# Input projections of ten column chunks as block products: seven products for eight

## The chip, the cores and the metric

The kernel runs on one core of one Trainium2 chip. A core has a tensor engine for matmuls (PE; its weight loads are listed as PEld), a vector engine (VectorE, DVE), a scalar engine (ScalarE, ACT), GpSimd (POOL) and SyncE (SP), which here issues nearly all transfers. Each engine runs its own instructions in a fixed order. Matmuls add up in eight banks of PSUM, of 512 fp32 numbers in each of 128 partitions; everything else lies in SBUF. The metric is the device time of one execution in microseconds.

## The reference

One layer of an encoder runs over two independent inputs with shared weights: a prompt of 512 tokens and a sample of 1024 tokens, 1024 features each, all in fp32. Cut to what matters here:

```
h = rmsnorm(x) ; z = h @ w_in                    # 1024 -> 512 q, 128 k, 128 v, 512 ca, 512 cb
a = window_attention(q, k, v, bias, sink)        # |q - k| <= 128
c = silu(layernorm(dwconv31(ca * sigmoid(cb))))  # over tokens, per channel
x = x + concat(a, c) @ w_out
u = dwconv3(rmsnorm(x) @ w_up)                   # 1024 -> 2 * 2816
x = x + (silu(u[:, :2816]) * u[:, 2816:]) @ w_down
y = rmsnorm(x)
```

The change concerns `z = h @ w_in` alone.

## The kernel before

**Numbers and tiles.** Every fp32 operand of a matmul is split in two: a leading part that ScalarE rounds to the format the tensor engine reads, and the remainder. A product is then three matmuls (leading by leading, leading by remainder, remainder by leading), each of 128 x 128 weights against 512 tokens. `split` makes the two parts of a weight chunk: ScalarE casts, GpSimd subtracts.

**The input projection.** The 1792 columns of `w_in` are 14 chunks of 128 columns. The tokens are three groups of 512: group 0 is the prompt, groups 1 and 2 are the halves of the sample. The activations come in transposed, x times the norm's gain is split by `raw_h1` (a cast on ScalarE, the remainder on VectorE) into `h1[group]`, and the norm's scale of each token is applied later, when a result leaves PSUM (`row_scale` makes it, `rbs` holds it). A step, one chunk for one group, is 8 blocks of 128 features by 3 matmuls, 24 in all (`proj`), after which `landed` and `evac` take the result out of its bank: VectorE scales it, and by its kind (q, k, v, ca, cb) it goes to the attention's buffers or to the input of the depthwise convolution.

**Order of the work.** `order` lists the chunks in two passes. In the first, the first two chunks (cb and ca of channel chunk 0) are done for all three groups as the data arrive (`beside`, line 526). Chunks 2 and 3 (channel chunk 1) follow for all three groups, and the ten others (k, v, four of q, and cb and ca of channel chunks 2 and 3) for group 0 alone. In the second pass these ten chunks are loaded and split again, for groups 1 and 2, while the prompt's attention runs beside them. Then come the prompt's output projection, its feed-forward part with the sample's attention beside it, the sample's output projection, its up-projection and the down-projection.

The prompt's convolutions run beside the first pass, mainly as a chain of 26 VectorE instructions for each channel chunk that multiply and add into one PSUM bank (`taps`, line 352), with four taps given to ScalarE and GpSimd. They are emitted by `tick`, which is called four times in a step: each call gives a credit (`CA`, 0.9 us in the first pass, `CB`, 0.4 us in the second), and a tap costs 0.663 us of credit. The side work of the second pass, the prompt's attention, is paced in the same way by a rate per tick (`RB`).

**What sets the order.** The text of the kernel gives each instruction its place in the program. A planner simulates the engines and gives each engine, whenever it is free, the earliest instruction in the program whose inputs and buffer are ready; that fixes the order of each engine's instructions. Late parts of the kernel have the tensor engine's order written out by hand (`manual_schedule`); the parts touched here do not. Buffers are slots of fixed sizes (`Slots`: classes q of 4096 bytes, h of 2048 and others), given out in the order of the program, oldest released first. The PSUM banks go the same way.

**The scheme that is there already.** The sample's up-projection (`prod`, `sums_up`, `split_up`, from line 1156) computes a product of 2 x 2 blocks with seven block products in place of eight: sums and differences of blocks are made on VectorE, and results are combined in PSUM by copying a bank into another as its starting value and adding further products to it. [...]

The lines that the change touches: 40 (`RB`), 122 (slots), 170 to 173 (`order`), 478 (`raw_h1`), 508 (`step`), 537 (`load_xT(2)`), 583 to 616 (the first pass), 897 to 905 (the second pass) and 1810 (the program's set-up).

Of the kernel before, what the change touches and what calls it, by code (L numbers as in the profile page):

```python
# [15 lines left out]
P = 128  # L16
# [22 lines left out]

RA, RB, RBO, RD, RN, RE = 1.2, 0.8, 2.5, 0.55, 0.8, 0.9  # L40

# [67 lines left out]
def tile_hybrid_encoder(ctx: ExitStack, tc: tile.TileContext, xs, rel_bias, norm_attn_g, w_in,  # L109
# [19 lines left out]
    def bank(job):  # L129
        return banks.tile([NT], among=use[job])  # L130
# [40 lines left out]
    npr = len(order)  # L171
    order += kv_ + qs + cs[2] + cs[3]
    nch = len(order)
    raws, ws = {}, {}

# [73 lines left out]
    lng, lnb, fb = vecs[:, 20:24], vecs[:, 24:28], vecs[:, 28:72]  # L249

    def square_sum(x, ss, k):
        junk = sb.tile([D], BF16, 2)
        if k % 2 == 0:
            nc.scalar.activation(junk[:], x[:], AF.Square, accum_out=ss)
        else:
            nc.vector.tensor_tensor_reduce(out=junk[:], in0=x[:], in1=x[:], scale=1.0, scalar=0.0,
                                           op0=ALU.mult, op1=ALU.add, accum_out=ss)

    def spread(rs, job):
        wide_rs = sb.tile([4, P])  # L260
        for i in range(4):
            nc.scalar.activation(wide_rs[:, i, :], ident[:], AF.Identity, scale=0.0, bias=rs[:, i:i + 1])
        pt = bank(job)
        for i in range(4):
            nc.tensor.transpose(pt[:, i * P:(i + 1) * P], wide_rs[:, i, :], ident[:])
        return pt
# [128 lines left out]
    def evac(kind, c, nt, src):  # L395
# [55 lines left out]
        else:  # L451
            vs = sb.tile([NT])
            nc.vector.tensor_tensor(vs[:], src, rb[:], op=ALU.mult)
            pt = bank("step")
            for i in range(4):
                nc.tensor.transpose(pt[:, i * P:(i + 1) * P], vs[:, i * P:(i + 1) * P], ident[:])
# [20 lines left out]

    def raw_h1(nt, kc):
        t, m = xq.pop((nt, kc))
        x, hi, lo = t[:, m, :], sb.tile([NT], F32R), sb.tile([NT], F32R)  # L480
        nc.scalar.activation(hi[:], x, AF.Identity, scale=gA[:, kc:kc + 1])
        nc.vector.scalar_tensor_tensor(lo[:], x, gA[:, kc:kc + 1], hi[:].bitcast(F32), op0=ALU.mult, op1=ALU.subtract)
        h1.setdefault(nt, []).append((hi, lo))

    def first_pieces():
        ws[0], ws[1] = [(Halves([]), Halves([])) for _ in range(2)]
        for (k0, n), w in zip(PIECES, first_w):
            hi, lo = sb.tile([n, 2 * P], F32R), sb.tile([n, 2 * P], F32R)
            for kc in range(k0, k0 + n):
                raw_h1(0, kc)  # L490
# [17 lines left out]
    def step(i, nt):  # L508
        kind, c, col = order[i]
        pp = bank("step")  # L510
        proj(pp[:], ws[i], h1[nt])
        landed(i, nt, pp)
# [23 lines left out]
    nc.sync.dma_start(cvw[:, :CK * 4], laid["cvw"])  # L536
    drawn(load_xT(2))
    want_raw(2)
# [9 lines left out]
    for kc in range(KC):  # L548
        raw_h1(1, kc)

# [32 lines left out]
    pace.update(rate=RA, conv=CA, late=0)  # L583
    NALL = 4
    for nt in range(3):
        if nt:
            pps.update({(nt, c): bank("step") for c in range(2)})
            for kc in range(KC):
                beside(nt, kc)
        if nt == 1:  # L590
            for kc in range(KC):
                raw_h1(2, kc)
            want_w(2)
            row_scale(1)
            want_raw(3)
            drawn(load_rows(2))
            constants()
        if nt == 2:
            row_scale(2)
            want_w(3)  # L600
        for i in range(2):
            landed(i, nt, pps.pop((nt, i)))
    for i in range(2):
        ws.pop(i)
    for i in range(2, npr):
        want_raw(i + 2)
        want_w(i + 1)
        for nt in range(3 if i < NALL else 1):
            step(i, nt)
        ws.pop(i)  # L610
        if i == 2:
            bbd = bias_to_dram()
        if i == BL:
            load_bias(2)
    drain(side)
    h1.pop(0)
    rbs.pop(0)
    blocks = [(G, b) for G in GR for b in range(G["nb"])]
# [1211 lines left out]
```

## Time and profile before

| what | value |
|---|---|
| median of 3 runs | 1486.21 us (1485.44 to 1487.02) |
| the profiled execution | 1484.85 us, its span 1483.1 us |
| busy: PE, PEld | 1468.5, 1212.0 us |
| busy: VectorE, ScalarE, GpSimd | 1118.2, 805.5, 770.7 us |
| mean granted clock of the tensor engine | 0.998 |
| chunks 0 and 1 (L526) | 4.9 to 39.3 us |
| first and second pass, other chunks (L315 to L317) | 39.3 to about 264 us |

In the answers of the profile an instruction stands with its line, engine and operation, the tile it writes and those it reads (`h<-q` writes a tile of slot class h and reads one of class q; a, b, c and u are PSUM banks), and its shape. A group shows the count, the busy time and the mean duration in ns, then the idle time of the engine just before these instructions and what ended it. In an order of time the first two numbers are start and duration in us, and a count behind x joins neighbours of one kind. A wait shows who waited for whom, the total in us, how often, and the longest.

### The profile page before, as it was taken

Reading aid. Unit: us, or ns where it says so; the run is one execution under the profiler, and the core shown is the slowest. Engines: PE = TensorE matmul, PEld = TensorE weight load, DVE = VectorE, ACT = ScalarE, POOL = GpSimd, SP = SyncE. Lnnn points to the kernel's source line nnn. Section 1 sums busy time; section 2 is a strip of 40 time slices with the busy share of each in tenths; the row PEclk is TensorE's granted clock in tenths of the full one; section 3 lists DMA queues with packets and bytes.
Section 4 is the critical chain, followed back from the end, with each engine's and each line's share of the span. In section 5 each row is a group of like instructions: output and inputs, shape, how many; then the busy total and the mean of one; then the engine's idle time right before and its main releaser. Section 6 shows DMA issues by size and latency. Waiting matters only on the chain.

```text
span 1483.1 us, 19870 instructions
## 1 busy us (share of the span) xinstructions
PE 1468.5 (99%) x6736; PEld 1212.0 (82%) x6736; DVE 1118.2 (75%) x1510; ACT 805.5 (54%) x1424; POOL 770.7 (52%) x689
## 2 busy tenths in 40 slices
PE   9999999999999999999999999999999999999998
PEld 7788887878888888788888888888888888888886
DVE  6877945648988888676868888888886856578774
ACT  7524555567778776653465545445544553433355
POOL 3564453338779766322336666666654251135546
PEclk9999999999999999999999999999999999999999
DMA  9554331844444454663214443333332494356644
GB/s 367 200 151 146 102 107 29 263 142 142 127 137 136 134 178 142 201 225 108 71 58 142 135 135 128 127 130 128 123 126 87 152 326 167 124 188 220 224 163 163
DMA packets 124626, 228.19 MB, mean 154 GB/s; under 512 B 20420, under 2 KB 45764, under 8 KB 124397
## 3 DMA queue, kind: packets, MB, share of 16 engines
q1 hardware_dynamic: 124092, 226.37, 46.6%
q8 instruction: 53, 0.87, 0.2%
q10 hardware_dynamic: 432, 0.56, 0.1%
q14 instruction: 49, 0.39, 0.1%
HBM read 166.83 MB, written 61.10 MB: 154 GB/s over the span
## 4 chain that ended last, share of the span: by engine, by line
PE 89%; DVE 3%; DMA 3%; ACT 2%; POOL 2%; issue 1%; SPq 0%; POOLq 0%; DVEq 0%; ACTq 0%
PE w L1194 8%; PE w L1196 8%; PE w L1195 8%; PE w L1528 7%; PE w L1527 7%; PE w L1526 7%; PE b L315 4%; PE b L317 4%; PE b L316 4%; PE u L315 4%; PE u L317 4%; PE u L316 4%; PE a L692 1%; PE a L650 1%; PE u L796 1%; PE u L798 1%
## 5 line engine op out<-in xcount | busy, mean ns | idle before, releaser
L163 POOL TENSOR_TENSOR q<-q,q 128x1024 fp32r<-128x1024 f32 x66 | 159.2, 2412 | 66.9 <-ACT q L162 42.8
L1074 POOL TENSOR_TENSOR q<-q,q 128x512 fp32r<-128x512 f32 x81 | 116.5, 1445 | 119.4 <-ACT q L1180 117.1
L1074 DVE TENSOR_TENSOR h<-h,h 128x512 fp32r<-128x512 f32 (+1 forms) x152 | 131.9, 897 | 57.6 <-ACT h L1082 23.4
L1526 PE MATMUL w<-h,h 128*128 128x512 f32 x432 | 168.0, 389 | 0.0
L1528 PE MATMUL w<-h,h 128*128 128x512 f32 x432 | 168.0, 389 | 0.0
L1527 PE MATMUL w<-h,h 128*128 128x512 f32 x412 | 160.3, 389 | 0.0
L1194 PE MATMUL w<-h,q 128*128 128x512 f32 x368 | 144.3, 392 | 0.7 <-ACT w L1267 0.4
L1196 PE MATMUL w<-h,q 128*128 128x512 f32 x368 | 143.2, 389 | 0.0
L1195 PE MATMUL w<-h,q 128*128 128x512 f32 x347 | 135.0, 389 | 0.0
L1074 POOL TENSOR_TENSOR h<-h,h 128x512 fp32r<-128x512 f32 (+1 forms) x38 | 53.5, 1411 | 142.4 <-ACT h L1509 117.5
L1082 ACT CAST h<-h 128x512 fp32r<-128x512 f32 x116 | 69.3, 620 | 104.4 <-DVE h L1074 25.8
L315 PE MATMUL b<-h,q 128*128 128x512 f32 x312 | 123.0, 395 | 1.4 <-ACT h L461 0.8
L317 PE MATMUL b<-h,q 128*128 128x512 f32 x312 | 122.5, 393 | 0.0
L316 PE MATMUL b<-h,q 128*128 128x512 f32 x312 | 122.3, 392 | 0.0
L315 PE MATMUL u<-h,q 128*128 128x512 f32 x272 | 106.8, 393 | 0.0
L316 PE MATMUL u<-h,q 128*128 128x512 f32 x272 | 106.8, 393 | 0.0
L317 PE MATMUL u<-h,q 128*128 128x512 f32 x272 | 106.7, 392 | 0.0
L162 ACT CAST q<-q 128x1024 fp32r<-128x1024 f32 x66 | 69.1, 1048 | 52.1 <-PE u L316 16.8
L352 DVE SCALAR_TENSOR_TENSOR c<-d,cvw,c 128x512 f32<-128x512 f32 x128 | 96.0, 750 | 1.6
L344 POOL TENSOR_TENSOR h<-h,h 128x512 f32<-128x512 f32 x62 | 81.6, 1318 | 27.5 <-ACT h L343 23.0
L1526 PEld LDWEIGHTS w<-h,h 128*128 128x128 f32 x432 | 81.1, 188 | 16.8
L1528 PEld LDWEIGHTS w<-h,h 128*128 128x128 f32 x432 | 81.1, 188 | 16.7
(474 smaller groups left out, 3990.3 us busy)
## 6 DMA issues: line engine op xcount, KB each, us to landing
q<-in_laid_w_up SPq DMA_DIRECT2D x88, 512.0 KB, 3.7
ga<-q SPq DMA_DIRECT2D x65, 256.0 KB, 2.2
h<-gap SPq DMA_DIRECT2D x57, 256.0 KB, 3.5
h<-ga SPq DMA_DIRECT2D x57, 256.0 KB, 3.5
h<-in_w_down SPq DMA_DIRECT2D x52, 256.0 KB, 3.4
q<-in_laid_w_in SPq DMA_DIRECT2D x22, 512.0 KB, 3.9
gap<-h SPq DMA_DIRECT2D x44, 256.0 KB, 3.2
q<-in_x_sample SPq DMA_DIRECT2D x15, 512.0 KB, 7.5
```

Of the source, the lines that this page charges most:

```text
L163: (nc.vector if dve else nc.gpsimd).tensor_tensor(lo[:], raw[:], hi[:].bitcast(F32), op=ALU.subtract)
L315: nc.tensor.matmul(out, whi[:, kc, :], hi[:], start=(kc == 0), stop=False)
L316: nc.tensor.matmul(out, whi[:, kc, :], lo[:], start=False, stop=False)
L317: nc.tensor.matmul(out, wlo[:, kc, :], hi[:], start=False, stop=(kc == KC - 1))
L352: nc.vector.scalar_tensor_tensor(acc[:], src(t), w(t), acc[:], op0=ALU.mult, op1=ALU.add)
L1074: (eng or nc.vector).tensor_tensor(out, a, b, op=ALU.subtract)
L1194: nc.tensor.matmul(out, whi[:, s], hi[:], start=(start and c == 0), stop=False, **go)
L1195: nc.tensor.matmul(out, whi[:, s], lo[:], start=False, stop=False, **go)
L1196: nc.tensor.matmul(out, wlo[:, s], hi[:], start=False, stop=(stop and c == 3), **go)
L1526: nc.tensor.matmul(out, sh[:, c], th[:], start=(p == 0 and not seeded), stop=False, **go)
L1527: nc.tensor.matmul(out, sh[:, c], tl[:], start=False, stop=False, **go)
L1528: nc.tensor.matmul(out, sl[:, c], th[:], start=False, stop=(p == NPAIR - 1), **go)
```

## The change

The ten chunks 4 to 13 become five pairs (k and v; q 0 and 1; q 2 and 3; cb and ca of channel chunk 2; of 3). For each pair the 2 x 2 blocks are: the two halves of the 1024 features, the two chunks, and the two token groups 0 and 1. `block_pair` computes the four results of a pair (two chunks for two groups) with seven block products of 4 x 3 matmuls.

- `x_sums` and `x_split` make the sums of x once: per feature block a difference on GpSimd, a scaling on ScalarE and three instructions on VectorE, then casts on ScalarE and remainders on GpSimd (on VectorE for operand 7). Products 1, 2 and 4 take parts of `h1` as they are. This stands between the four plain steps of chunks 2 and 3 and in the first pair.
- `w_sums` and `w_split` make the sums of a pair's weights (four instructions on VectorE) and split the seven operands (seven casts on ScalarE, seven remainders on GpSimd, of 512 elements), one pair ahead.
- `seeded` copies a bank into another by ScalarE as its starting value, with an additional matmul if the bank is in `cut_banks`, that is, if it was last cleared by a transpose.
- Group 2 leaves the first pass. Its loads move: the rows for the norm to the third pair, the transposed activations to the last, where `raw_h1` splits them. The second pass does all 14 chunks for group 2 only, 14 steps; four more chunks of weights are loaded and split again.
- `load_bias` moves behind the pairs. `RB` goes from 0.8 to 1.15. Seven slots of class h are added, and the set-up reserves less memory for descriptors of transfers.

The core of the diff:

```diff
-RA, RB, RBO, RD, RN, RE = 1.2, 0.8, 2.5, 0.55, 0.8, 0.9
+RA, RB, RBO, RD, RN, RE = 1.2, 1.15, 2.5, 0.55, 0.8, 0.9
-               dict(q=(15, 4096), c=(4, 4352), h=(61, 2048), d=(2, 2304), s=(33, 64)))
+               dict(q=(15, 4096), c=(4, 4352), h=(68, 2048), d=(2, 2304), s=(33, 64)))
-    order += kv_ + qs + cs[2] + cs[3]
+    order += kv_ + qs + cs[0] + cs[1] + cs[2] + cs[3]
+    PLAIN = 4
+    pairs = [(i, i + 1) for i in range(PLAIN, npr, 2)]
...
+    def x_sums(c):
+        g1, g2 = gA[:, c:c + 1], gA[:, HK + c:HK + c + 1]
+        x11, x21, x12, x22 = x_of(0, c), x_of(0, HK + c), x_of(1, c), x_of(1, HK + c)
+        d = xsum[7, c] = sb.tile([NT])
+        nc.gpsimd.tensor_tensor(d[:], x11, x12, op=ALU.subtract)
+        nc.scalar.activation(x12, x12, AF.Identity, scale=g1)
+        nc.vector.scalar_tensor_tensor(x12, x22, g2, x12, op0=ALU.mult, op1=ALU.add)
+        nc.vector.scalar_tensor_tensor(x11, x11, g1, x12, op0=ALU.mult, op1=ALU.subtract)
+        nc.vector.scalar_tensor_tensor(x21, x21, g2, x11, op0=ALU.mult, op1=ALU.add)
...
+    def w_sums(p):
+        if p < len(pairs):
+            g0, g1, v0, v1 = (w_block(i, k) for i in pairs[p] for k in range(2))
+            t = wthird[p] = sb.tile([NT])
+            tt = nc.vector.tensor_tensor
+            tt(t[:], v1, v0, op=ALU.subtract)
+            tt(v0, v0, g0, op=ALU.subtract)
+            tt(g0, v0, v1, op=ALU.subtract)
+            tt(g1, g1, g0, op=ALU.add)
...
+    def block_prod(out, p, i, start):
+        whi, wlo = wops.pop((p, i))
+        for c in range(HK):
+            hi, lo = xop[i, c]
+            s = slice(c * P, (c + 1) * P)
+            nc.tensor.matmul(out, whi[:, s], hi[:], start=(start and c == 0), stop=False, **go)
+            nc.tensor.matmul(out, whi[:, s], lo[:], start=False, stop=False, **go)
+            nc.tensor.matmul(out, wlo[:, s], hi[:], start=False, stop=(c == HK - 1), **go)
+            if c == 1:
+                tick()
+        tick()
...
+    def seeded(src):
+        out = bank("step")
+        if out.slot[0] in cut_banks:
+            hi, lo = xop[5, HK - 1]
+            nc.tensor.matmul(out[:], hi[:, 0:P], hi[:], start=True, stop=True)
+            cut_banks.discard(out.slot[0])
+        nc.scalar.copy(out[:], src[:])
+        return out
...
+    def block_pair(p):
+        a, b = pairs[p]
+        last = p == len(pairs) - 1
+        w_load(p + 2)
+        X = started()
+        block_prod(X[:], p, 1, True)
+        Y = seeded(X)
+        if p == 0:
+            for c in range(HK):
+                x_split(7, c)
+            w_split(p, 7)
+        else:
+            w_split(p + 1, 1, 2)
+            w_sums(p + 1)
+        block_prod(X[:], p, 2, False)
+        if last:
+            drawn(load_xT(2))
+        landed(a, 0, X)
...
+        block_prod(Y[:], p, 6, False)
+        u = sb.tile([NT])
+        nc.scalar.copy(u[:], Y[:])
...
+        Z = started()
+        block_prod(Z[:], p, 5, True)
+        p5 = sb.tile([NT])
+        nc.scalar.copy(p5[:], Z[:])
+        w_split(p + 1, 7)
+        block_prod(Y[:], p, 7, False)
+        V = seeded(Y)
+        nc.vector.tensor_tensor(Y[:], Y[:], p5[:], op=ALU.add)
...
+        block_prod(Z[:], p, 3, False)
+        nc.vector.tensor_tensor(Z[:], Z[:], u[:], op=ALU.add)
...
+        block_prod(V[:], p, 4, False)
+        landed(a, 1, V)
+        landed(b, 0, Z)
+        landed(b, 1, Y)
...
-    for i in range(2, npr):
-        want_raw(i + 2)
-        want_w(i + 1)
-        for nt in range(3 if i < NALL else 1):
-            step(i, nt)
-        ws.pop(i)
+    w_load(0)
+    for n, (i, nt) in enumerate(((2, 0), (2, 1), (3, 0), (3, 1))):
+        if n == 2:
+            w_split(0, 1, 2)
+            w_sums(0)
+        x_sums(n)
+        for k in (6, 5):
+            x_split(k, n)
+        step(i, nt)
...
+    w_split(0, 6, 5)
+    for p in range(len(pairs)):
+        if p == len(pairs) - 3:
+            drawn(load_rows(2))
+            row_scale(2)
+        block_pair(p)
+    load_bias(2)
...
-        for nt in range(1, 3):
-            step(i, nt)
+        step(i, 2)
...
-    nc = _bacc.Bacc("TRN2", target_bir_lowering=False, num_devices=1)
+    nc = _bacc.Bacc("TRN2", target_bir_lowering=False, num_devices=1, dynamic_dma_scratch_size=1024)
```

More of the change, by code (lines that the diff above doesn't have):

```diff
@@ L249, in tile_hybrid_encoder @@
     lng, lnb, fb = vecs[:, 20:24], vecs[:, 24:28], vecs[:, 28:72]
+    cut_banks = {f[0] for f in banks.free}
     def square_sum(x, ss, k):
@@ L263, in spread @@
         pt = bank(job)
+        cut_banks.add(pt.slot[0])
         for i in range(4):
@@ L454, in evac @@
             pt = bank("step")
+            cut_banks.add(pt.slot[0])
             for i in range(4):
@@ L548, in tile_hybrid_encoder, with pair_tile, x_of @@
     for kc in range(KC):
-        raw_h1(1, kc)
+        raw_h1(1, kc, True)
+    HK = KC // 2
+    xop, wops, wdone, wthird = {}, {}, set(), {}
+    def pair_tile():
+        if sum(f[0][0] == "q" for f in sb.free) > 6:
+            both = sb.tile([2, NT], F32R, among="q")
+            return Part(both, 0), Part(both, 1)
+        return sb.tile([NT], F32R), sb.tile([NT], F32R)
+    xsum = {}
+    def x_of(nt, kc):
+        t, m = xq[nt, kc]
+        return t[:, m, :]
+    def x_sums(c):
[7 more added lines that the diff above has]
+        nc.vector.scalar_tensor_tensor(x21, x21, g2, x11, op0=ALU.mult, op1=ALU.add)
+        xq.pop((1, HK + c))
@@ new lines, in x_split @@
+    def x_split(i, c):
+        hi, lo = xop[i, c] = pair_tile()
+        if i == 7:
+            src, g = xsum.pop((7, c))[:], gA[:, c:c + 1]
+            nc.scalar.activation(hi[:], src, AF.Identity, scale=g)
+            nc.vector.scalar_tensor_tensor(lo[:], src, g, hi[:].bitcast(F32), op0=ALU.mult, op1=ALU.subtract)
+            return
+        key = {5: (1, c), 6: (0, c), 3: (0, HK + c)}[i]
+        src = x_of(*key)
+        nc.scalar.copy(hi[:], src)
+        nc.gpsimd.tensor_tensor(lo[:], src, hi[:].bitcast(F32), op=ALU.subtract)
+        xq.pop(key)
@@ new lines, in w_split @@
+    def w_split(p, *which):
+        if p >= len(pairs):
+            return
+        a, b = pairs[p]
+        for i in which:
+            if i == 7:
+                held = wthird.pop(p)
+                src = held[:]
+            else:
+                src = w_block(*{1: (a, 0), 2: (a, 1), 6: (a, 0), 4: (a, 1), 5: (b, 0), 3: (b, 1)}[i])
+            if any(f[0][0] == "q" for f in sb.free):
+                t = sb.tile([2, NT], F32R, among="q")
+                hi, lo = Part(t, 0), Part(t, 1)
+            else:
+                hi, lo = sb.tile([NT], F32R), sb.tile([NT], F32R)
+            wops[p, i] = hi, lo
+            nc.scalar.copy(hi[:], src)
+            nc.gpsimd.tensor_tensor(lo[:], src, hi[:].bitcast(F32), op=ALU.subtract)
+            held = None
+            wdone.add((p, i))
+        for chunk, two in ((a, (6, 4)), (b, (5, 3))):
+            if chunk in raws and all((p, i) in wdone for i in two):
+                raws.pop(chunk)
@@ new lines, in block_prod @@
+    def block_prod(out, p, i, start):
+        whi, wlo = wops.pop((p, i))
+        go = dict(skip_group_check=not start)
+        for c in range(HK):
[4 more added lines that the diff above has]
+            nc.tensor.matmul(out, wlo[:, s], hi[:], start=False, stop=(c == HK - 1), **go)
+            if p == len(pairs) - 1:
+                xop.pop((i, c))
+            if c == 1:
+                tick()
+        tick()
```

93 lines of the change are left out of this document (65 added, 28 removed).

## The prediction

> **What bounds the kernel now.** I read the page first, then the tensor engine in order of time, then busy time by stretch, then the groups of instructions in the stretch that the change rebuilds.
>
> ```profile
> PE 1468.5 (99%) x6736; PEld 1212.0 (82%) x6736; DVE 1118.2 (75%) x1510; ACT 805.5 (54%) x1424; POOL 770.7 (52%) x689
> PE 89%; DVE 3%; DMA 3%; ACT 2%; POOL 2%; issue 1%; SPq 0%; POOLq 0%; DVEq 0%; ACTq 0%
> L526 PE MATMUL a<-h,h 128*128 128x512 f32 x48 | 11.0, 389 | 0.0
> 17.04 11.04 PE L526 MATMUL a<-h,h 128*128 128x512 f32 x48
> ```
>
> The tensor engine is busy for 1468.5 of 1483.1 us and carries 89% of the chain, so a matmul fewer is time saved, if the others keep up. What one is worth is not its duration. The last line is 48 matmuls back to back in 11.04 us; one alone lasts 0.389 us, so the pitch is (11.04 - 0.389) / 47 = 0.2266 us. I count with the pitch.
>
> ```profile
> 0.00:17.00 17.00, 15.32 (x64) 11.88 (x65) 8.90 (x13) 12.08 (x19) 7.50 (x22) 1.00 0.89 315
> 25.60:69.00 43.40, 42.73 (x191) 34.13 (x191) 39.06 (x58) 26.01 (x46) 20.45 (x17) 1.00 0.66 247
> 128.00:264.00 136.00, 133.45 (x653) 110.40 (x652) 90.43 (x182) 73.34 (x163) 60.41 (x77) 1.00 0.30 87
> 830.00:1100.00 270.00, 270.00 (x1190) 222.53 (x1189) 228.35 (x199) 134.46 (x200) 168.97 (x127) 1.00 0.40 131
> 1470.00:1483.10 13.10, 7.25 (x32) 5.66 (x31) 2.79 (x3) 2.95 (x7) 3.50 (x4) 0.86 0.57 220
> ```
>
> Columns: the stretch, its length, busy time of PE, PEld, DVE, ACT and POOL with their instructions, granted clock, DMA share, GB/s. The clock is 1.00 in all that the change touches. The tensor engine loses 1.7 us at the start and 5.9 at the end; elsewhere it hardly waits. But from 25.6 to 69.0 us the vector engine is busy for 39.06 of 43.4 us. That is where the change puts its preparation, and the argument turns on it.
>
> **The work removed.** A pair of column chunks for the prompt and the first sample group takes four steps of 24 matmuls, 96. Seven block products of 12 take 84. Five pairs save 60: 60 x 0.2266 = 13.6 us. The second sample group's steps are only moved. A bank last cleared by a transpose costs an extra matmul before it is seeded; following the banks in their order of release I find one such (the fourth of the second pair): 0.2 us, with 0 to 10 of them (2.3 us) as ends.
>
> **The start of the block products.** The first fence's last line ends at 28.1 us with both chunks of the first sample group done. Four plain steps (96 x 0.2266 = 21.8) reach 49.9, the first pair (84, 19.0 us) 68.9: by then every block operand of x and of the first pair's weights must exist. So I budget 25.6 to 69.0.
>
> ```profile
> L352 DVE SCALAR_TENSOR_TENSOR c<-d,cvw,c 128x512 f32<-128x512 f32 x26 | 19.6, 754 | 0.6
> L482 DVE SCALAR_TENSOR_TENSOR h<-q,vecs,h 128x512 fp32r<-128x512 f32 x8 | 5.6, 751 | 2.2 <-ACT h L481 2.2
> L256 DVE CUSTOM_DVE_ANT_0 d<-q 128x1024 bf16<-128x1024 f32 x2 | 2.5, 1230 | 0.0
> L424 DVE SCALAR_TENSOR_TENSOR c<-d,a 128x512 f32<-128x512 f32 x1 | 1.1, 1117 | 0.0
> L416 DVE TENSOR_TENSOR a<-a,h 128x512 f32<-128x512 f32 x1 | 0.7, 690 | 0.0
> L163 POOL TENSOR_TENSOR q<-q,q 128x1024 fp32r<-128x1024 f32 x5 | 12.0, 2402 | 14.1 <-ACT q L162 14.0
> L147 POOL TENSOR_TENSOR s<-s,nhalf 128x4 f32<-128x4 f32 x3 | 3.5, 1171 | 0.1
> ```
>
> ```profile
> L1074 DVE TENSOR_TENSOR q<-q,q 128x512 f32<-128x512 f32 x21 | 22.2, 1059 | 0.2
> L1071 DVE TENSOR_TENSOR w<-w,h 128x512 f32<-128x512 f32 x28 | 19.5, 695 | 5.4 <-ACT w L1285 3.4 <-PE w L1196 1.2
> L1074 POOL TENSOR_TENSOR q<-h,q 128x512 fp32r<-128x512 f32 x14 | 18.1, 1292 | 0.0
> L1074 POOL TENSOR_TENSOR c<-q,c 128x512 fp32r<-128x512 f32 x35 | 56.7, 1628 | 21.5 <-ACT c L1180 21.2
> L1180 ACT CAST q<-q 128x512 fp32r<-128x512 f32 x50 | 31.1, 623 | 35.1 <-PE w L1196 19.8 <-DVE h L1074 11.9 <-DVE q L1331 3.4
> ```
>
> These are groups with count, busy time and mean ns: the first fence from 25.6 to 69.0 us, the second from 830 to 1100, where the sample's up-projection already does the same kinds of sums, splits and additions into PSUM for a seven-product scheme.
>
> Vector engine: 39.06 now. Out go the eight remainders of the second sample group (5.6) and its two squares (2.5). In come two additions into PSUM (2 x 0.695 = 1.4), one more pair of evacuations (L416 and L424, 1.8), and 24 instructions that read two SBUF tiles: twelve sums of x, four remainders of operand 7, eight sums of weights (the first two pairs). The price of one lies between 0.751 (L482, two SBUF inputs, GpSimd idle for much of its time) and 1.059 (L1074, GpSimd busy): 18.0 to 25.4. Together 52.2 to 59.6 us, with no more conv taps than now, against 43.4: 8.8 to 16.2 too much.
>
> GpSimd: 20.45, less three of the five full weight splits (7.2) and one inverse root (1.2), plus 23 operations on 512 elements (4 differences, 12 remainders of x, 7 of weights) at 1.292 to 1.628: 41.8 to 49.5. It is full as well. ScalarE gains 23 casts of 0.623 and a few copies, loses as many full casts and squares, goes from 26.0 to about 35, and is not the limit.
>
> What hides the excess: the planner gives the tensor engine whatever is ready, and the first two products of the next pair use operands with no sum in them (24 x 0.2266 = 5.4 us). So I expect a stall of 8.8 - 5.4 = 3.4 to 16.2 - 5.4 = 10.8 us and take the middle, 7. It shows first as a wait of products 6 and 7 for remainders of x; queued behind on the tensor engine are the pair's products 3 and 4, then the second pair, whose banks come free later. Nothing makes it good afterwards, since the tensor engine has no slack.
>
> [...]
>
> **Loads.** Eight 512 KB loads of the second sample group leave the first 41 us for the third and fifth pair, and four more weight chunks are loaded and split in the second pass.
>
> ```profile
> 17.00:28.00 11.00, 11.00 (x50) 9.09 (x50) 8.28 (x14) 7.72 (x15) 2.94 (x4) 1.00 1.05 408
> 20.17 0.34 SPq L156 DMA_DIRECT2D q<-in_laid_w_in  x1
> 23.67 0.68 POOL L146 TENSOR_SCALAR s<-s 128x4 f32<-128x4 f32 x1 [10.02 <-DVE cvw L542]
> ```
>
> The third chunk's weights are now wanted at 28.1 instead of 39.3 us. Their load was issued on SP at 20.17 behind four of those loads, which at 408 GB/s are 2.1 MB / 0.408 = 5.1 us, so they land that much sooner; GpSimd stood idle for 10 us before 23.67, so their split (2.4) fits there. I cost this at nothing; if the split comes behind the last x operand, about 1 us.
>
> **The steady pairs.** In 19.0 us a pair needs 4 weight sums (4 x 1.06 = 4.2), 2 additions (1.4) and some 5 of evacuation on the vector engine, and up to 11 remainders (7 of weights, 4 of q: 17.9 at 1.628) on GpSimd. It fits; with a like load PE was busy 270 of 270 us. One dependency is new: product 2 adds into the bank that ScalarE is copying as the seed of Y.
>
> ```profile
> PE w L1194 <- ACT w L1267: 0.4, 1, 0.4
> PE u L707 <- DVE q L695: 0.9, 2, 0.7
> ACT h L663 <- DVE s L654: 32.0, 12, 9.0
> ```
>
> The like copy in the up-projection cost 0.4 us once (first line). Five pairs: 0 (product 5 of the same pair fills in) to 2.0; I take 0.7.
>
> **The second pass.** Twenty steps become fourteen; the 136 us of the third row above lose 6 x 24 x 0.2266 = 32.6 and become 103, under which the whole prompt attention has to run (its rate goes from 0.8 to 1.15 per tick, over 56 ticks for 80, so the same number of items). Vector engine 90.4 less six evacuations and some taps done earlier, about 78 of 103; GpSimd 60.4 and four more splits (9.6), 70; ScalarE 73.3 and four casts, 77. None is full. The tensor engine waited 2.6 us there, most for the attention's chain (the 0.9 above); a third denser, I add 0.9, with 0 and 3 as ends.
>
> **The sum.** -13.6 + 0.2 + 7 + 0.7 + 0.9 = -4.8 us on the profiled execution's 1484.85 (span 1483.1 and 1.75 around it): 1480.05. The median of the runs shown, 1486.21, lies 1.36 above that execution, so I forecast 1481.4.
>
> **Rivals.**
>
> *The backlog is absorbed.* The planner places an instruction as soon as its inputs are there, and the vector engine has gaps before 30 us (the 2.2 idle of L482). If the sums of x slip into them and taps give way, only the 0.2 and about 0.5 of waits remain: 1486.2 - 13.6 + 0.7 = 1473.3. Against it: both VectorE and GpSimd are over full by count.
>
> *Taps go first (slower).* Conv taps are handed out by ticks, 0.9 us of credit each, and a pair now gives 18 ticks. By the end of the first pair 38 ticks have passed, 34.2 us of credit or 51 taps at 0.663; the stretch now holds 28, first and last operation counted. The 23 more cost 23 x 0.754 = 17.3 us on the vector engine ahead of later sums and evacuations. If half of it reaches the tensor engine, the stall is 7 + 8.7 = 15.7 and the time 1490. It turns into a loss when the stall passes 13.6 - 0.2 - 0.7 - 0.9 = 11.8, and a measurable one at 14.8. Against it: chunk 1 can begin only when chunk 0's accumulator is done, and most of the 23 come behind product 7's operands.
>
> [...]
>
> *The attention loses its cover.* If every one of its eight units costs a further wait of the 0.7 us seen for L707, 5.6 in all for the 0.9: 1486.1. For it: from 128 to 330 us ScalarE waited 32 us for its scores (third line of the last fence). Against it: steps are there to fill in.
>
> **How the numbers follow.** About 0.2% (3 us) is what a measurement of this kernel tells from no change: faster ends at 1483.2, slower begins at 1489.2. Forecast 0.48 (stalls of 3.4 to 10.8 and the other ends give 1476 to 1488.6: 0.29 faster, 0.15 the same, 0.04 by luck of the ends slower), backlog absorbed 0.22, taps first 0.14, port 0.05, attention 0.11 (0.03, 0.07, 0.01). Faster 0.29 + 0.22 + 0.03 = 0.54; same 0.15 + 0.05 + 0.07 = 0.27; slower 0.04 + 0.14 + 0.01 = 0.19. The range reaches from the absorbed case to the taps, 1472.5 to 1490.5.
>
> **What would show it.** Block products at a pitch of 0.227, 420 of them with one seed; PE idle of some 7 us between 50 and 100 us, ended by VectorE or GpSimd operands of x, and next to none from the second pair to 145; VectorE over 90% busy from 25 to 90 us; the second pass shorter by about 33 us with PE idle under 5. [...]

## The result: 6.4% slower, and where the time went

The changed kernel takes 1580.55 us (median of four runs, 1578.97 to 1582.35), the kernel before 1485.89 (four runs, 1485.44 to 1487.02). The ratio is 1.0636, its 95% interval 1.0618 to 1.0655. I had forecast 1481.4 and a range up to 1490.5. The matmuls did go: the page of the changed kernel counts 6677 for 6736, which is the 60 taken out and the one additional matmul.

```profile
PE 1489.2 (94%) x6677; PEld 1213.4 (77%) x6677; DVE 1143.5 (72%) x1556; ACT 836.4 (53%) x1493; POOL 835.1 (53%) x734
PE 67%; DVE 14%; DMA 5%; issue 5%; ACT 5%; POOL 3%; SPq 0%; POOLq 0%; ACTq 0%; DVEq 0%
```

The tensor engine's part of the chain falls from 89% to 67%, and it is idle for 91 us of its span, where it was for 15. Busy time by stretch shows where. Columns: the stretch, its length, busy time of PE, PEld, DVE, ACT and POOL with their instructions, granted clock, DMA share, GB/s. First the changed kernel:

```profile
0.00:50.00 50.00, 36.07 (x144) 28.85 (x145) 41.89 (x44) 31.99 (x54) 34.65 (x42) 0.91 0.69 256
50.00:100.00 50.00, 48.02 (x206) 38.24 (x205) 48.35 (x65) 25.45 (x47) 37.73 (x29) 0.96 0.37 110
100.00:150.00 50.00, 34.47 (x134) 26.65 (x133) 28.86 (x39) 19.89 (x38) 26.60 (x21) 0.83 0.47 134
150.00:200.00 50.00, 40.88 (x173) 32.67 (x172) 35.38 (x46) 22.26 (x37) 26.60 (x31) 0.93 0.49 147
300.00:350.00 50.00, 37.53 (x151) 27.89 (x150) 30.75 (x55) 28.37 (x61) 14.16 (x17) 0.80 0.43 133
900.00:1200.00 300.00, 285.11 (x1230) 228.37 (x1228) 216.29 (x207) 136.16 (x205) 161.56 (x129) 1.00 0.36 119
```

Then the kernel before:

```profile
0.00:50.00 50.00, 47.64 (x210) 38.38 (x210) 37.94 (x57) 34.61 (x58) 18.49 (x31) 1.00 0.87 331
50.00:100.00 50.00, 50.00 (x223) 40.39 (x222) 41.19 (x58) 20.19 (x31) 29.00 (x23) 1.00 0.53 158
100.00:150.00 50.00, 50.00 (x234) 41.69 (x233) 35.64 (x65) 20.24 (x41) 26.04 (x25) 1.00 0.55 163
150.00:200.00 50.00, 48.67 (x237) 40.29 (x236) 38.64 (x73) 27.40 (x60) 25.43 (x31) 1.00 0.31 91
300.00:350.00 50.00, 48.62 (x239) 39.22 (x238) 31.50 (x67) 36.63 (x77) 28.02 (x32) 1.00 0.44 151
900.00:1200.00 300.00, 299.64 (x1320) 246.91 (x1319) 242.38 (x225) 149.62 (x223) 162.52 (x122) 1.00 0.41 136
```

Count matmuls, not busy time: from 337 to 341 us of the changed kernel, at a granted clock of 0.50, 10 of them keep PE busy for all 4 us, and from 341 to 345, at 0.99, 19 do. At the pitch of 0.2266 us the deficits are 83 matmuls before 100 us (18.8 us), 164 from 100 to 200 (37.2), 88 from 300 to 350 (19.9) and 90 from 900 to 1200 (20.4). The last is the sample's up-projection, which no line of the change touches. These four places are the largest, and I looked for a cause at each. Some 12 matmuls are missing from 350 to 400 us too, and 42 (9.5 us) from 600 to 900 (1361 for 1403). The waits of PE in the changed kernel, total, times, longest:

```profile
PE w L1380 <- ACT w L1453: 14.7, 16, 3.4
PE b L644 <- ACT q L630: 13.0, 1, 13.0
PE b L320 <- ACT h L512: 8.4, 1, 8.4
PE a L644 <- ACT d L694: 6.9, 1, 6.9
PE u L879 <- ACT h L856: 4.2, 1, 4.2
```

In this order: the up-projection (L1380) waits for a seed copy; a block product waits for the cast of its weights; a plain step for the copy of the first sample group's row scales; a block product of a later pair for the copy of a result (6.9 us, at 170 us); the attention's transposes for a softmax. The second is worth following. Its chain, in order of time (start, duration, what), is not about weights at all:

```profile
126.63 2.39 DMA qsd<-h
...
129.12 0.63 ACT h L434
...
130.40 2.38 DMA qsd<-h
...
132.93 0.63 ACT h L434
...
134.20 2.40 DMA qsd<-h
...
136.70 0.07 ACT h L258
...
139.03 0.52 ACT q L630
...
139.61 1.28 POOL q L631
...
140.94 0.80 PE b L646
```

A q result is copied by ScalarE into an h slot (L434) and transferred out of it (`qsd`, 2.4 us). The next instruction that is given this slot waits for the transfer, three times in a row, the third time a square of the norm (L258). In ScalarE's order the cast that PE needs (L630) stands behind them all and starts at 139.03 us. Following the allocation in the program's text, class h (2048 bytes) has at most two free slots of 68 at the end of each of the first four pairs and none at its tightest. A slot is then given out again almost as soon as it is released: 20 of the 159 requests in the pairs get one that was released at one of the two requests before. From this came the first theory.

**Theories.** *Slots in the pairs*: class h is exhausted, reuse waits for transfers and late readers. *Rotation*: the seven added slots shift which slots are given out in all later stages, and that costs the up-projection. *Overload*, nearest to my forecast: VectorE and GpSimd have too much to do. *Cover*: the prompt's attention lost work that hid it.

### The profile page after: what moved, and what is told of

Its sections match the earlier page's. It is cut to its first block, busy times and chain, and to the rows that moved or that the text cites. A ratio compares the mean times of both kernels' runs of the same rounds, so it can differ in the third digit from the quotient of the medians.

```text
span 1580.5 us, 19886 instructions
## 1 busy us (share of the span) xinstructions
PE 1489.2 (94%) x6677; PEld 1213.4 (77%) x6677; DVE 1143.5 (72%) x1556; ACT 836.4 (53%) x1493; POOL 835.1 (53%) x734
## 4 chain that ended last, share of the span: by engine, by line
PE 67%; DVE 14%; DMA 5%; issue 5%; ACT 5%; POOL 3%; SPq 0%; POOLq 0%; ACTq 0%; DVEq 0%
PE w L1712 6%; PE w L1713 6%; PE w L1714 6%; PE w L1380 4%; PE w L1382 4%; PE w L1381 4%; PE u L321 3%; PE u L320 3%; PE u L322 3%; PE b L320 3%; PE b L322 3%; PE b L321 3%; DVE q L1260 2%; PE a L837 2%; DVE c L357 1%
## 5 line engine op out<-in xcount | busy, mean ns | idle before, releaser
L1260 POOL TENSOR_TENSOR q<-q,q 128x512 fp32r<-128x512 f32 x118 | 168.5, 1434 | 153.2 <-ACT q L1366 153.0
L1380 PE MATMUL w<-h,q 128*128 128x512 f32 x560 | 221.8, 396 | 19.2 <-ACT w L1453 14.7
L1381 PE MATMUL w<-h,q 128*128 128x512 f32 x560 | 218.7, 390 | 0.0
L1382 PE MATMUL w<-h,q 128*128 128x512 f32 x560 | 218.7, 390 | 0.0
L1714 PE MATMUL w<-h,h 128*128 128x512 f32 x452 | 175.9, 389 | 0.0
L1713 PE MATMUL w<-h,h 128*128 128x512 f32 x452 | 175.8, 389 | 0.0
L1712 PE MATMUL w<-h,h 128*128 128x512 f32 x452 | 175.8, 389 | 0.0
L163 POOL TENSOR_TENSOR q<-q,q 128x1024 fp32r<-128x1024 f32 x60 | 145.0, 2419 | 58.1 <-ACT q L162 25.1
L1380 PEld LDWEIGHTS w<-h,q 128*128 128x128 f32 x560 | 105.5, 188 | 51.4 <-ACT w L1453 21.5
L1382 PEld LDWEIGHTS w<-h,q 128*128 128x128 f32 x560 | 105.4, 188 | 22.4
L1381 PEld LDWEIGHTS w<-h,q 128*128 128x128 f32 x560 | 105.5, 188 | 21.0
L357 DVE SCALAR_TENSOR_TENSOR c<-d,cvw,c 128x512 f32<-128x512 f32 x154 | 115.4, 750 | 1.8
L320 PE MATMUL b<-h,q 128*128 128x512 f32 x240 | 96.3, 403 | 8.4 <-ACT h L512 8.4
L1499 DVE SCALAR_TENSOR_TENSOR q<-w,fw,q 128x1023 f32<-128x1023 f32 x43 | 55.0, 1280 | 65.2 <-ACT q L1498 65.0
L1714 PEld LDWEIGHTS w<-h,h 128*128 128x128 f32 x452 | 84.8, 188 | 17.7
L1712 PEld LDWEIGHTS w<-h,h 128*128 128x128 f32 x452 | 84.8, 188 | 17.7
L321 PE MATMUL u<-h,q 128*128 128x512 f32 x248 | 98.3, 396 | 0.0
L1713 PEld LDWEIGHTS w<-h,h 128*128 128x128 f32 x452 | 84.8, 188 | 17.4
L320 PE MATMUL u<-h,q 128*128 128x512 f32 x248 | 98.2, 397 | 0.0
```

The source lines that it names most:

```text
L163: (nc.vector if dve else nc.gpsimd).tensor_tensor(lo[:], raw[:], hi[:].bitcast(F32), op=ALU.subtract)
L320: nc.tensor.matmul(out, whi[:, kc, :], hi[:], start=(kc == 0), stop=False)
L321: nc.tensor.matmul(out, whi[:, kc, :], lo[:], start=False, stop=False)
L357: nc.vector.scalar_tensor_tensor(acc[:], src(t), w(t), acc[:], op0=ALU.mult, op1=ALU.add)
L1260: (eng or nc.vector).tensor_tensor(out, a, b, op=ALU.subtract)
L1380: nc.tensor.matmul(out, whi[:, s], hi[:], start=(start and c == 0), stop=False, **go)
```

## Experiments

Times are of one run, or the median where several were made; a run of the kernel before on the same chip took 1484.4 to 1486.5 each time. Differences under about 3 us are not read.

### Two set-up lines alone

```diff
 # kernel before
-    ... h=(61, 2048) ...
+    ... h=(68, 2048) ...
-    nc = _bacc.Bacc("TRN2", ..., num_devices=1)
+    nc = _bacc.Bacc("TRN2", ..., num_devices=1, dynamic_dma_scratch_size=1024)
```

> The kernel before with two set-up lines of the change only: 68 slots of class h for 61, and the smaller reserve for descriptors. Not one matmul is added or removed. Theory 'rotation': with seven more h slots the allocator no longer spills into classes c, d and q in the later stages, other slots are handed out again there while a transfer or a slow reader still holds them, and the up-projection of the sample loses what it lost in the changed kernel (about 117 matmuls in 350 us, some 26 us): 1510 us, with the loss between 850 and 1200 us. Rival 'only the new work costs': 1485 to 1487 us, no PE idle time there.

> The kernel before with the smaller reserve for descriptors and nothing else (61 slots). It tells apart the two set-up lines that cost 39.5 us together. Theory 'rotation': 1485 to 1488 us. Rival 'reserve': about 1526 us.

With both lines the kernel before takes 1526.03 us, 39.5 more; with the smaller reserve alone 1485.89. So seven more slots, used by nobody new, cost some 40 us. In its up-projection, busy time by stretch and PE's first wait are those of the changed kernel:

```profile
900.00:1200.00 300.00, 289.89 (x1253) 233.33 (x1252) 219.99 (x214) 144.77 (x218) 157.30 (x124) 1.00 0.39 129
PE w L1194 <- ACT w L1267: 14.7, 16, 3.4
```

Not all of it lies there: 25 matmuls are missing in the first 100 us too, and 34 from 200 to 300.

### The seven slots given back

```diff
     out = deque([prompt_out()])
+    for _ in range(7):
+        sb.free.remove(next(f for f in reversed(sb.free) if f[0][0] == "h"))
```

> The changed kernel, with seven of its h slots taken out of use from the prompt's output projection on, so that the later stages have 61 as before. The first 300 us are unchanged. Theory 'rotation': the up-projection of the sample is as dense as before, the run is 20 to 28 us shorter than the changed kernel: 1553 to 1560 us. Rival 'the late loss comes from the earlier delay or from the smaller reserve': 1578 to 1583 us.

> The changed kernel with seven h slots taken out of use at the end of the pairs, ahead of the second pass, instead of at its end. Theory 'rotation' holds for all stages behind the pairs: then the 44 us of the run that gave them back at the output projection are reached again or passed (1525 to 1537 us), and PE's loss from 200 to 400 us becomes smaller if it came from slots too; if that loss comes from the lost cover alone, it stays at some 90 matmuls and the time at 1534 to 1538.

Given back at the output projection: 1536.19 us, 44.4 less than the change, which is more than expected. The up-projection is as before, its stretch full:

```profile
900.00:1200.00 300.00, 299.63 (x1321) 247.13 (x1320) 247.08 (x216) 150.09 (x221) 182.60 (x134) 1.00 0.37 123
```

The same lines one stage earlier, at the end of the pairs (ahead of `load_bias(2)`): 1539.89, and PE has 166 matmuls from 300 to 350 us where 176 were (239 in the kernel before). So it is not these seven slots that the second pass suffers from; its loss has another cause.

### Which tiles it is

The allocator gives the smallest free slot that is large enough, the longest free first. In the up-projection of the kernel before, so many requests of 2048 bytes overflow into larger classes that 68 of 291 tiles of 4096 bytes fall to the four slots of class c (4352 bytes). With seven more h slots only 11 do; c lies idle and these tiles rotate over q, where the convolution's copies (L1498) meet slots that are still being transferred.

```diff
 # dwconv of the up-projection, changed kernel with all its slots
-        u = sb.tile([W2])
+        u = sb.tile([W2], among="c" if any(s[0][0] == "c" for s in sb.free) else None)
```

> The changed kernel with all its 68 h slots; only the scaled copies that the convolution of the sample's up-projection makes (one tile of 4096 bytes each) take a slot of class c where one is free, as most did by chance in the kernel before. No instruction is added or removed. Theory 'rotation': ScalarE's copy into such a tile no longer waits for a transfer out of the slot, PE no longer waits for the seed copy behind it (14.7 us in 16 waits), and most of the 44 us come back: 1538 to 1553 us. Rival 'it is the slots of class h as such' (or the place in SBUF): 1575 to 1582 us.

1557.62 us: 22.9 less than the change, 5 to 20 short of what I expected in all. Where the theory speaks, it holds. One thing in my expectation is wrong: in the kernel before 18 of the 44 convolution copies lay in c, not most of them (1 in the changed kernel, all 44 here). So this run shows that a place in c takes the waits away; it does not restore the places of the kernel before. The waits that went, first in the changed kernel:

```profile
ACT w L1453 <- DVE q L1500: 39.4, 16, 6.5
ACT q L1498 <- DMA ga<-q: 11.0, 8, 2.7
```

and what is left of PE's wait with the tiles in c, with the stretch:

```profile
PE w L1380 <- ACT w L1453: 0.6, 1, 0.6
900.00:1200.00 300.00, 298.10 (x1313) 245.93 (x1312) 237.84 (x219) 148.46 (x220) 179.20 (x136) 1.00 0.38 127
```

The other 21.4 us that giving back the slots had won lie mostly between 300 and 900 us (with the slots given back PE has 411 matmuls from 300 to 400 us for 377 here, and from 700 to 800 us 507 for 451); which tiles it is there was not tried.

### Slots in the pairs

```diff
 # first pair, operand 3 of x
             for c in range(HK):
-                x_split(3, c)
+                xop[3, c] = xop[6, c]; xq.pop((0, HK + c))     # first run
+                x_split(3, c); xop[3, c] = xop[6, c]           # second run
```

> The changed kernel, but operand 3 of x is not made: product 3 reads operand 6's two tiles (so part of the result is left out). Four casts on ScalarE and four remainders on GpSimd fall away in the first pair, and eight slots of class h stay free from there on; the matmuls are the same. Theory 'slots': the loss between 100 and 200 us (37 us) is q results, weight operands and sums waiting for the one h slot that a 2.4 us transfer or a late reader still holds; with 5 to 6 slots free at the tightest place most of it goes: 25 to 37 us less, 1544 to 1556 us. Rival 'overload' (VectorE and GpSimd have too much to do in the pairs): the eight operations are 4 x 0.62 + 4 x 1.7 us of the first pair alone, at most 9 us less: 1571 us or more, and the loss between 100 and 200 us stays.

> As the run that left operand 3 of x out, but its four casts and four remainders are made (and read by nobody): product 3 reads operand 6, so part of the result is left out. The work of every engine is that of the changed kernel, only eight h slots stay free. Theory 'slots': 1552 to 1556 us, as without the work. Theory 'overload': those eight operations were the gain, and it goes back to 1575 us or more. In between, the share of each is read off.

1552.33 and 1552.46 us. The eight operations cost nothing; the eight free slots are worth 28 us. Busy time by stretch of the second run, with the same work as the changed kernel:

```profile
100.00:150.00 50.00, 47.46 (x203) 38.42 (x202) 36.97 (x51) 23.93 (x44) 35.19 (x32) 0.97 0.65 192
150.00:200.00 50.00, 48.53 (x229) 39.97 (x228) 47.36 (x83) 30.41 (x62) 30.16 (x33) 1.00 0.50 162
```

432 matmuls from 100 to 200 us for 307, and the wait of 13 us is gone. Product 3 no longer depends on operand 3 in these runs, but that is not what won: in the changed kernel operand 3 is complete at 88.2 us, and PE works without a gap from 65.7 to 94 us. These two runs settle the second place.

```diff
 # slots won by a move: the loads of the pair after next
     def block_pair(p):
-        w_load(p + 2)
...
         block_prod(Y[:], p, 7, False)
+        w_load(p + 2)
```

> The changed kernel with the weight loads of the pair after next issued behind product 7 instead of ahead of product 1. Two q slots are then free through most of a pair, the weight operands lie in them, and of 159 requests in the pairs none gets a slot released at one of the last two requests, where 20 did. No work is left out. Theory 'slots': most of the 28 us that came from leaving operand 3 out: 1553 to 1562 us, PE with 400 or more matmuls from 100 to 200 us (305 in the changed kernel). Rival 'less work in the first pair': 1575 to 1582 us. If the later loads themselves come late, PE waits for casts behind a load at the start of a pair.

1568.64 us, 11.9 less: the direction is right, the size less than half of what eight free slots bring. PE has 339 matmuls from 100 to 200 us, and the wait for the cast of weights is 4.7 us for 13.0. Requests that get a slot released within the last two are gone, but 46 of 157 still get one released within the last eight; in the first of the two runs above it was 4. My measure of when reuse is harmless was too mild.

Both slot effects together:

```diff
+                x_split(3, c); xop[3, c] = xop[6, c]
+    for _ in range(7): sb.free.remove(...)      # at the output projection
```

> The changed kernel with product 3 reading operand 6 (operand 3 made, but read by nobody, so part of the result is left out; eight h slots free in the pairs), and the seven slots given back at the output projection. If the two effects of slots lie in different stages, 1580.5 - 28.1 - 44.4 = 1508 us, 1504 to 1513. If they are partly one loss, 1520 us or more, as the three edits together gave less than their sum.

1508.82 us. They add to within a microsecond: 71.7 us of the loss is slots. Of these, 22.9 are followed to their tiles and some 28 to the pairs; the other 21 are shown only as an effect of the seven slots behind the pairs.

### The cover of the second pass

```diff
-RA, RB, ... = 1.2, 1.15, ...
+RA, RB, ... = 1.2, 1.7, ...
```

> The changed kernel with the rate of the prompt's attention in the second pass at 1.7 for 1.15 per tick. Theory 'cover': the loss of some 20 us between 300 and 350 us comes because the attention's last units are still to be done when the steps run out; paced faster they end beside steps and 10 to 20 us go: 1560 to 1570 us. Rival 'loads': the output projection waits for its weights, whose loads are issued at 305.6 us when the steps have given back their slots: then it stays within 3 us of 1580.

1573.17 us, 7.4 less, between the two. From 200 to 300 us PE loses 35 matmuls, from 300 to 400 it gains 60: of what a faster rate wins at the end, more than half is lost ahead of it.

```diff
 # last six steps of the second pass; RB 0.8, seven slots given back
+        if i >= nch - 6:
+            pp = bank("step"); proj(pp[:], ws[i], h1[2]); pp = None; tick()
         step(i, 2)
```

> The changed kernel with the seven slots given back (1536.2) and six more steps in the second pass, beside its last six steps: 144 matmuls into a bank that nobody reads, 144 x 0.2266 = 32.6 us of tensor work, with the attention's rate at 0.8, so that the second pass has 20 steps and 80 ticks as before the change. Theory 'cover': the attention's end and the start of the output projection have work beside them again, 15 to 20 us of PE's idle time are filled, and the run is only 13 to 18 us longer: 1549 to 1554 us. If the stall has other causes (the w_out loads, slots), it stays: 1566 to 1570 us.

1557.04 us: 32.6 us of tensor work added cost 20.8, so 11.8 of it ran in time that was idle (the attention's rate went back to 0.8 in the same run). That is less than I expected, but the place is right. From 250 to 350 us the tensor engine is now busy throughout:

```profile
250.00:300.00 50.00, 50.00 (x249) 42.09 (x248) 26.65 (x56) 26.81 (x57) 25.25 (x24) 1.00 0.29 86
300.00:350.00 50.00, 50.00 (x249) 41.61 (x248) 26.58 (x46) 22.46 (x49) 14.69 (x18) 1.00 0.40 120
```

### The preparation of x

```diff
 # no sums, no splits; seven slots given back
-        x_sums(n)
-        for k in (6, 5): x_split(k, n)
...
+        xop[6, c], xop[3, c], xop[5, c], xop[7, c] = h1[0][c], h1[0][HK + c], h1[1][c], h1[1][HK + c]
```

> The changed kernel with the seven slots given back, and without any preparation of x: products 3, 5, 6 and 7 read tiles of the plain operands (so part of the result is left out). 16 casts, 16 remainders, four differences, four scalings and twelve sums fall away, and 24 h slots are free. Weights and matmuls are as in the change. Theory: the preparation of x costs the first 150 us some 15 to 19 us beyond the slots (28.1): 1536.2 - 28.1 - 17 = 1491 us, 1487 to 1496, and PE has 430 or more matmuls in the first 100 us. Rival 'the pairs themselves do it' (weight sums, seeds, evacuations): as with slots alone, 1504 to 1510 us.

1495.71 us, 40.5 less than with the preparation: 27.4 for the slots (as above) and 13.1 beyond them, though 16 more slots are free here and may have a part in that. The first 50 us are those of the kernel before, 209 matmuls for 210; from 50 to 150 us still 64 are missing:

```profile
0.00:50.00 50.00, 48.43 (x209) 38.89 (x210) 36.72 (x51) 32.80 (x57) 28.21 (x40) 1.00 0.84 316
50.00:100.00 50.00, 47.14 (x205) 38.56 (x204) 47.39 (x65) 24.60 (x46) 32.17 (x29) 0.97 0.43 120
100.00:150.00 50.00, 44.86 (x188) 36.24 (x187) 33.04 (x46) 27.28 (x48) 30.91 (x26) 0.93 0.59 174
```

How does the preparation cost that? In the changed kernel the sums of x stand on VectorE before 50 us, ahead of work that PE wants first. Groups of VectorE from 25.6 to 69.0 us (count, busy time, mean ns), then single instructions of VectorE and GpSimd (start, duration):

```profile
L580 DVE SCALAR_TENSOR_TENSOR h<-h,vecs,h 128x512 f32<-128x512 f32 x4 | 6.8, 1724 | 0.0
L357 DVE SCALAR_TENSOR_TENSOR c<-d,cvw,c 128x512 f32<-128x512 f32 x9 | 6.8, 751 | 0.2
L579 DVE SCALAR_TENSOR_TENSOR h<-h,vecs,q 128x512 f32<-128x512 f32 x3 | 5.4, 1814 | 0.1
L578 DVE SCALAR_TENSOR_TENSOR q<-q,vecs,q 128x512 f32<-128x512 f32 x3 | 4.3, 1470 | 0.0
```

```profile
43.51 0.74 DVE L578 SCALAR_TENSOR_TENSOR q<-q,vecs,q 128x512 f32<-128x512 f32 x1
44.35 2.93 DVE L579 SCALAR_TENSOR_TENSOR h<-h,vecs,q 128x512 f32<-128x512 f32 x1
```

```profile
44.38 2.35 POOL L163 TENSOR_TENSOR q<-q,q 128x1024 fp32r<-128x1024 f32 x1
```

The same kind of instruction takes 0.74 us before GpSimd's long subtraction starts, and 2.93 when it runs from 44.38 to 46.73: it ends 0.55 us after that. A tap (L357), which adds into PSUM and so reads one SBUF tile, keeps its 0.751 us (0.754 in the kernel before). GpSimd's instruction was no longer than in the kernel before: 2.35 us, for a mean of 2.402 there.

```diff
 # all four squares of the first sample group on ScalarE
-        if k % 2 == 0:
+        if k % 2 == 0 or nt == 1:
```

> The changed kernel with all four squares of the first sample group on ScalarE (two were on VectorE). Before 50 us PE stands 8.4 us for the copy of that group's row scales; its last square ran on VectorE at 42.4 us behind sums of x that took 1.5 to 2.9 us each for 0.75. Theory 'the sums of x come ahead of what PE waits for next': the wait of 8.4 us goes or falls under 3, and the run is 3 to 8 us shorter: 1572 to 1577 us. Rival 'VectorE is the limit as a whole up to 70 us': PE waits as long a little later, 1578 us or more.

1584.08 us. PE's wait for the row scales fell from 8.4 to 3.0, about as expected, and nothing was won: the first 100 us have 356 matmuls for 350, the next 100 us 294 for 307. Here a wait taken away, in a stretch that is full, came back behind it.

```diff
 # differences and remainders of x; seven slots given back
-        nc.gpsimd.tensor_tensor(...)
+        nc.vector.tensor_tensor(...)
```

> The changed kernel with the seven slots given back (1536.2) and GpSimd's part of the x operands (four differences and twelve remainders) on VectorE: some 12 us more there, 26 us less on GpSimd. Theory 'port': VectorE's operations on two SBUF tiles, 1.5 to 2.9 us beside GpSimd's, come back to 0.75 us, VectorE's busy time is no longer in the first 100 us, and the run is 1525 to 1536 us. Theory 'VectorE has too much to do': 12 us more work come out as 5 to 12 us more time: 1541 to 1548 us.

1544.65 us, 8.5 more than with them on GpSimd. Both theories have a part. L580 and L579 come down, but to 1.26 and 1.09 us, not 0.75 (the other subtractions of GpSimd remain). The start gets denser by it, 366 matmuls in the first 100 us for 350. The loss lies behind it, from 100 to 150 us, with 96 matmuls for 134, at the wait of the pairs for a weight cast, 20.8 us for 12.9. There 14 taps run in a row from 117.00 to 128.07 us, ahead of the next evacuation of q (from 24 to 90 us 20 taps ran, for 26 in the changed kernel). As far as these rows show, the work added to VectorE costs its time there, not at the start:

```profile
L580 DVE SCALAR_TENSOR_TENSOR h<-h,vecs,h 128x512 f32<-128x512 f32 x4 | 5.0, 1262 | 0.0
L579 DVE SCALAR_TENSOR_TENSOR h<-h,vecs,q 128x512 f32<-128x512 f32 x3 | 3.3, 1088 | 0.0
```

```profile
PE b L644 <- ACT q L630: 20.8, 1, 20.8
```

```diff
-CA, CB = 0.9, 0.4
+CA, CB = 0.3, 0.9
```

> The changed kernel with the taps of the prompt's convolution handed out at a third of the pace in the first pass (0.3 for 0.9 of credit per tick) and faster in the second (0.9 for 0.4). Some 25 taps of 0.754 us leave VectorE's work between 30 and 210 us. Theory 'overload' (VectorE's sums and evacuations come late behind other work): PE's 305 matmuls from 100 to 200 us become 340 or more, and the first 200 us gain 8 to 19 us, part of which may be lost again in the second pass: 1562 to 1576 us. Theory 'slots' alone: 300 to 315 matmuls there, 1578 us or more.

1579.31 us, no difference, and no test either. From 24 to 100 us VectorE still did 33 taps (31 in the changed kernel): the credit sets where a tap stands in the program, but the planner takes it forward when VectorE has nothing earlier that is ready.

### Fewer pairs, and edits together

```diff
-    PLAIN = 4
+    PLAIN = 10        # ten chunks in plain steps, x_sums beside the last four steps; slots given back
```

> The changed kernel with ten chunks in plain steps for both groups and only the last four (cb and ca of channel chunks 2 and 3) as two pairs of block products, the sums of x beside the last four plain steps; the seven slots given back as above (that version is at 1536.2). It has 36 matmuls (8.2 us) more. If the loss of the first 200 us comes from the start of the block products (sums of x beside the first group's norm, and q results in too few slots), most of its 60 us goes: 1490 to 1505 us. If every pair costs alike by its work, three pairs fewer of five: 1536 + 8 - 0.6 x 37 = 1522 us or more.

1514.25 us, 21.9 less than five pairs, though it has 8.2 us more of matmuls: 30 us of stall less. The first 100 us have 435 matmuls (433 in the kernel before); from 100 to 200 us, where its two pairs lie, there are 373 for 471. So the start of the block products costs there too, only less.

> The changed kernel with the later weight loads (-11.9 us alone), the seven slots given back at the output projection (-44.4) and the attention's rate at 1.7 (-7.4). If the three causes lie in different stages, as the theory has it, the gains add: 1580.5 - 63.7 = 1517 us, 1512 to 1522. Rival 'one loss seen three times': 1530 us or more.

1536.12 us: together the two other edits bring nothing once the slots are given back, so the gains of the edits do not add. Which of the two fails was not taken apart. Where that is seen: up to 400 us this run is 14 matmuls (3.2 us) ahead of the one that only gives back the slots, not 19 us. It wins 32 from 100 to 200 us by the later loads, loses 35 from 200 to 300 by the rate, and from 300 to 400 giving back the slots had already brought 36 of what the rate was to bring. These 3.2 us are lost again from 600 to 700 us, 463 matmuls for 477; by what was not found.

No version tried is faster than the kernel before.

## Why the prediction was wrong

**The account.** From 1486.2 - 13.6 + 0.2 = 1472.8 us to 1580.5 are 107.7. The runs show 71.7 for slots (44.4 in the stages behind, 27 to 28 in the pairs), 13.1 for the preparation of x (part of it perhaps for the 16 further slots that are free in that run), and 11.8 for lost cover, by what the added steps filled. The remaining 11 are not isolated; the run without x preparation still misses 64 matmuls (14.5 us) from 50 to 150 us, where its pairs are, so most of it may lie there.

**Right: the work removed.** 60 matmuls, one more for a seed, at the pitch read from the profile. The second pass is nearly as short as I said, from about 202 us to 309.7, 107 us for 103. PE's two waits for seed copies in the pairs (L659) came to 1.1 us, for 0.7 (0 to 2.0). One sum was off: with the extra matmuls at their end of 2.3 us the ends reach 1490.7, not 1488.6; nothing hangs on it.

**Wrong, and decisive: "seven slots of class h are added" had no term in the sum.** I listed it as part of the change and priced nothing. It is two things. In the pairs the operands of x alone take up to 56 slots of class h (seven operands, four feature blocks, two tiles each), so that with the seven added class h is still at its end, and every evacuation there waits for a transfer or a reader. Behind the pairs the same seven slots change the choice of slots in stages that the change does not touch. I had looked at engines, queues and banks, and the profile of before could not show either; the allocation could have been followed in the program's text, and was not.

**Wrong: the steady pairs, "it fits".** The counts of work did fit (VectorE is busy for 28.86 of 50 us from 100 to 150 us). What did not is the order: q results, squares and weight casts share ScalarE, and one that waits for a slot holds the rest. I forecast next to no PE idle time past the second pair, and there were 15.5 us from 100 to 150 alone.

**Mis-sized: the stall at the start, 7 us.** That VectorE is over full there is as forecast; where it shows is not. VectorE is full from 25.6 to 69.0 us, 42.8 of 43.4, and PE does 117 matmuls for 191 there. I priced an operation on two SBUF tiles at 0.751 to 1.059 us; the sums of x took 1.47 to 1.81. GpSimd's price for the same size, 1.292 to 1.628, was somewhat low (1.29 to 1.93 by group). And I had the wait at products 6 and 7, between 50 and 100 us. PE was idle for 13.9 us in the first 50 us (2.4 in the kernel before) and for 2.0 in the next; it waited for a remainder (4.1 us, at about 30 us) and for the row scales (8.4), as sums that were ready ran ahead of what PE needed, and the first pair's products then ran with hardly a gap. It came although only 9 taps ran in the stretch in place of 26. What this place costs by itself, 13.1 us, lies above my range of 3.4 to 10.8.

**Wrong: the second pass, 0.9 us (0 to 3).** Some 11.8. The rival that the attention loses its cover was the right mechanism, priced at 5.6 from single waits of 0.7 us. But the loss is not in the middle of the pass, where steps fill in: it is at its end, when the steps have run out and attention and output projection have nothing beside them.

**The other rivals.** Taps going first: refuted, there were fewer. Port, a loss on GpSimd's instructions, 0.05 in the sum of the chances: no run shows the term that it was priced by. What the runs showed in its place: the sums of x on VectorE took 1.47 to 1.81 us for 0.75, and GpSimd's operations 1.29 to 1.93 by group for 1.292 to 1.628. Absorbed backlog: its premise came true in part, three sums of x stand before 28 us and the taps gave way, and the stall came all the same. And my range allowed for no cause outside the stages that I had read.

## What to carry to other kernels

When a change alters a pool of buffers, follow the allocation from there to the end of the kernel, under the rule by which slots are given out: a pool at its end can turn a transfer out of a slot into a wait of an engine whose order is fixed (here three transfers of 2.4 us stood ahead of a wait of PE of 13.0), and a larger pool can be worse (39.5 us for seven slots), if a best-fit rule then stops using slots that had kept some tiles apart. Test it by changing the pool alone in the old kernel. A sum of work per engine says whether a stage can fit, not whether it does, and the last items of side work need cover as much as the first.

## What the runs showed of the hardware

Idle time cost more than itself in one place. The chain of the changed kernel after the stalls from 312 to 335 us:

```profile
336.74 0.80 PE u L984
337.53 0.43 PE u L985
...
340.52 0.43 PE u L983
340.95 0.34 PE u L984
341.29 0.23 PE u L985
```

For 4 us the matmuls follow each other at 0.43 us and then at 0.23. The granted clock was 0.50 from 337 to 341 us and 0.99 from 341 to 345. The mean granted clock from 300 to 350 us was 0.80, and over the whole run 0.975 for 0.998. A lower clock did not come with all idle time: from 900 to 1200 us PE is idle for 14.9 us, and the granted clock was 1.00. I had not put a lower clock into any price of a stall, and in the kernel before, with a granted clock of 1.00 in every stretch that the change touches, there was no row to read it from.

A VectorE instruction with two SBUF inputs took longer beside a GpSimd subtraction, in the rows above: 0.74 us before it, 2.93 beside it, and the subtraction 2.35.
